# SwiGLU gate and up projections with seven block products for eight, and the down projection as its own stage

## The chip, the cores and the metric

The kernel runs on one core of one Trainium2 chip. The metric is device time in microseconds. The kernel before took 2962.8 us (median of three runs, 2962.63 to 2965.72). Engines: TensorE (PE) multiplies, VectorE (DVE) and ScalarE (ACT) do elementwise work, GpSimd (POOL) does a little of it, SyncE (SP) issues the transfers. PSUM is where TensorE accumulates.

## The reference

One decoder layer in fp32 with 2048 tokens, D = 1024 and D_FF = 2816, in three residual sub-layers. The change is in the third; the others are a hybrid token mixer and a cross-attention into 256 memory tokens.

```
hf = rmsnorm(x, g_ffn_pre)
ff = (jax.nn.silu(hf @ w_gate) * (hf @ w_up)) @ w_down
x = x + rmsnorm(ff, g_ffn_post)
```

## The kernel before

Every fp32 operand of a large product is split into two parts, hi and lo, in the format fp32r: `split` casts on ACT (L142) and subtracts on DVE or, where told, on POOL (L143). A product is then three passes, hi by hi, hi by lo and lo by hi (`PASS`), all into the same PSUM accumulation. A matmul has a 128x128 weight and 512 columns.

The stages follow one another: input projection, differential attention, output projection (`pmix`, L870), cross-attention over 16 token tiles (`psc` L1056, `pxo` L1095), and last SwiGLU, called the last stage here. The order on TensorE is written out by hand; that of ACT, DVE, POOL and SP is a scheduler's, which follows data and buffers.

The last stage works on two halves of 1024 tokens, and on 22 blocks f of 128 of D_FF. The tokens of a half are normalised (`d_load`, L126), turned by eight transposes (`d_turn`, L132) and split into `hfT` (L134, L135). For each f, `gate_up` loads a 512 KB block of w_gate and of w_up, splits each, and runs for each two groups (512 tokens) of 24 matmuls, 8 contraction blocks by 3 passes (`gu_mm`, L1173): 96 matmuls per f and half, 4224 in all. `gu_post` takes Silu on ACT (L1178), multiplies on DVE (L1179) and splits g, with POOL. After every two f's `down` multiplies g by two blocks of w_down (L1203, 96 matmuls: eight token tiles by two groups of six), and adds the result to y in SBUF (L1215). At the end of each half `down_end` does the last four f's, normalises y, adds the residual (POOL, L1263) and stores it, and in the first half turns the tokens of the second between its matmuls.

The first blocks are woven into the end of cross-attention: four token tiles are turned within its last two tokens, the four others between the first gate and up matmuls. Loads go through four buffers (`raw`, name `wr`), split weights through ten (`w4`), PSUM is four buffers of 1024 columns (`ps`). Pools are on the left side of SBUF, save those made with `right`: among them `vwp` (VW of cross-attention) and `yp` (y and g).

## Time and profile before

| what | us |
|---|---|
| median of three runs | 2962.8 |
| lowest and highest | 2962.63, 2965.72 |
| span of the profiled execution | 2962.6 |
| TensorE busy in it | 2879.2 (97%) |
| DVE busy | 1312.5 (44%) |
| ACT busy | 966.4 (33%) |
| POOL busy | 278.9 (9%) |
| last stage, first gate matmul to the end | 1481.6 to 2962.6 |

The profile is one execution; its span is the time from the first to the last instruction, and the median of the runs agrees with it. A matmul's own duration in it (390 ns for the gate and up matmuls) overlaps with its neighbours'; what a matmul costs is the pitch, the time of a run in the chain of waits divided by its count. The chain is followed back from the last instruction: each piece says who held the end at that time. Times below count from the start of the span.

### The profile page before, as it was taken

How to read it: one execution, taken by the hardware profiler on the slowest of the kernel's cores; microseconds unless marked ns; L12 is line 12 of the kernel's file. 1: busy time of each engine (PE TensorE's matmuls, PEld its weight loads, DVE VectorE, ACT ScalarE, POOL GpSimd, SP SyncE). 2: the span in 40 equal slices, each digit the busy share in tenths (PEclk: the TensorE clock that was granted, in tenths of full speed). 3: DMA queues.
4: the chain of work that ended last, by engine and by line, in shares of the span. 5: the costliest groups of instructions: out<-in, count | busy, mean ns of one | idle time of the engine just before them, and what ended most of it. 6: DMA issues, size and time to landing. Idle time of an engine off the chain costs nothing.

```text
span 2962.6 us, 34656 instructions
## 1 busy us (share of the span) xinstructions
PE 2879.2 (97%) x13948; PEld 2384.2 (80%) x13948; DVE 1312.5 (44%) x2069; ACT 966.4 (33%) x1986; POOL 278.9 (9%) x183
## 2 busy tenths in 40 slices
PE   9989999999889999999999999999999999999998
PEld 7778778888777888888878888888877888888887
DVE  4362378787885554333531332222263133222224
ACT  4232247677774443222322111111132211111112
POOL 0000012221221000000000000000021000000002
PEclk9999999999999999999999999999999999999999
DMA  5443473543433541111221111111143111111112
GB/s 181 137 162 107 158 222 108 150 141 106 134 100 119 192 172 44 44 50 47 92 96 50 43 44 57 50 50 49 44 143 113 50 43 45 56 50 50 50 43 100
DMA packets 217752, 273.48 MB, mean 92 GB/s; under 512 B 12280, under 2 KB 167032, under 8 KB 217592
## 3 DMA queue, kind: packets, MB, share of 16 engines
q1 hardware_dynamic: 217272, 270.22, 28.7%
q8 instruction: 110, 1.80, 0.3%
q0 software_dynamic: 320, 1.05, 0.1%
q14 instruction: 50, 0.41, 0.0%
HBM read 206.09 MB, written 65.14 MB: 92 GB/s over the span
## 4 chain that ended last, share of the span: by engine, by line
PE 81%; DVE 7%; DMA 2%; ACT 2%; issue 2%; POOL 1%; SPq 0%; DVEq 0%; ACTq 0%; POOLq 0%
PE pgu L1173 32%; PE pdn L1203 15%; PE pxo L1095 6%; PE psc L1056 6%; PE pmix L870 5%; PE S L731 3%; PE o L792 3%; PE pu L287 2%; DVE p L773 2%; PE pqk L287 2%; DVE nmx L738 2%; PE pv L303 1%; PE T L783 1%; PE S L870 1%; PE o L537 1%
## 5 line engine op out<-in xcount | busy, mean ns | idle before, releaser
L1173 PE MATMUL pgu<-hfT,w 128*128 128x512 f32 x4224 | 964.6, 390 | 3.3 <-DVE ms_y L106 2.0
L1173 PEld LDWEIGHTS pgu<-hfT,w 128*128 128x128 f32 x4224 | 793.4, 188 | 170.0 <-DVE ms_y L106 2.4
L1203 PE MATMUL pdn<-wd,g 128*128 128x512 f32 x2112 | 497.5, 396 | 2.2 <-ACT pdn L1260 2.2
L1203 PEld LDWEIGHTS pdn<-wd,g 128*128 128x128 f32 x2112 | 398.5, 189 | 95.5 <-ACT pdn L1260 2.6
L142 ACT CAST w<-wr 128x1024 fp32r<-128x1024 f32 (+2 forms) x208 | 134.4, 686 | 760.8 <-PE pgu L1173 414.0
L143 DVE TENSOR_TENSOR w<-wr,w 128x1024 fp32r<-128x1024 f32 (+2 forms) x206 | 156.8, 794 | 258.8 <-ACT w L142 245.1
L143 POOL TENSOR_TENSOR g<-sg,g 128x1024 fp32r<-128x1024 f32 x42 | 101.0, 2404 | 1745.5 <-ACT g L142 1745.5
L1179 DVE TENSOR_TENSOR sg<-pgu,sg 128x1024 f32<-128x1024 f32 x44 | 53.9, 1225 | 416.5 <-PE pgu L1173 416.5
L1215 DVE TENSOR_TENSOR y<-pdn,y 128x1024 f32<-128x1024 f32 x128 | 156.8, 1225 | 180.7 <-PE pdn L1203 180.7
L731 PE MATMUL S<-kt,q 128*128 128x512 f32 (+2 forms) x640 | 180.7, 397 | 34.3 <-ACT p L747 32.5
L747 ACT ACTIVATE p<-S,nmx 128x1024 f32<-128x1024 f32 (+3 forms) x192 | 167.7, 874 | 93.4 <-DVE nmx L740 39.1
L738 DVE TENSOR_REDUCE nmx<-S 128x1 f32<-128x1024 f32 (+3 forms) x192 | 173.4, 908 | 45.3 <-PE S L734 34.9
L1095 PE MATMUL pxo<-VW,pT 128*128 128x512 f32 x768 | 183.3, 397 | 0.4 <-ACT pT L142 0.4
L287 PE MATMUL pqk<-hT,w 128*128 128x512 f32 x768 | 179.3, 395 | 3.8 <-ACT w L142 3.8
L1056 PE MATMUL psc<-Mq,h 128*128 128x512 f32 x768 | 178.9, 392 | 0.0
L287 PEld LDWEIGHTS pqk<-hT,w 128*128 128x128 f32 x768 | 144.5, 188 | 38.3 <-ACT w L142 4.6
L1095 PEld LDWEIGHTS pxo<-VW,pT 128*128 128x128 f32 x768 | 143.1, 188 | 33.4 <-ACT pT L142 0.6
L1056 PEld LDWEIGHTS psc<-Mq,h 128*128 128x128 f32 x768 | 143.0, 188 | 29.3
L731 PEld LDWEIGHTS S<-kt,q 128*128 128x128 f32 x640 | 110.9, 195 | 58.8 <-ACT p L747 43.2
L870 PE MATMUL pmix<-wo,in 128*128 128x512 f32 x624 | 145.2, 394 | 0.0
L870 PEld LDWEIGHTS pmix<-wo,in 128*128 128x128 f32 x624 | 117.0, 188 | 27.6
L792 PE MATMUL o<-vt,aT 128*128 128x128 f32 x1088 | 136.5, 280 | 0.0
(257 smaller groups left out, 2883.8 us busy)
## 6 DMA issues: line engine op xcount, KB each, us to landing
wr<-in_w_gate SPq DMA_DIRECT2D x44, 512.0 KB
wr<-in_w_up SPq DMA_DIRECT2D x44, 512.0 KB
wr<-in_w_down SPq DMA_DIRECT2D x44, 512.0 KB
wr<-in_w_in SPq DMA_DIRECT2D x32, 512.0 KB
q<-qk_q SPq DMA_DIRECT2D x128, 128.0 KB
xt<-in_x SPq DMA_DIRECT2D x16, 512.0 KB
wr<-in_w_xkv SPq DMA_DIRECT2D x16, 512.0 KB
kt<-qk_k SPq DMA_DIRECT2D x16, 512.0 KB
```

Source lines behind the costliest of these rows:

```text
L143: (eng or v).tensor_tensor(dst_lo, src, dst_hi, ALU.subtract)
L287: pe.matmul(pt[:, ch * 512:(ch + 1) * 512], w[ws][:, k, :], hT[ch][hs][:, k, :], start=(n == 0), stop=(n == 23))
L731: pe.matmul(st[:, c0:c0 + cwm], x["qs"][s][:, m, q0:q0 + P], x["kst"][m][pc][:, c0:c0 + cwm], start=(s == 0), stop=(s == 1 and not last))
L738: v.tensor_reduce(nmx[:, pc:pc + 1], st[:, :w_], AX.X, ALU.max, negate=True)
L747: sc.activation(pt[:, :w_], st[:, :w_], AF.Exp, bias=nmx[:, pc:pc + 1], accum_out=x["l2"][:, m, pc:pc + 1])
L792: pe.matmul(ot[:, :P], aT[b // 4][:, (b % 4) * P:(b % 4 + 1) * P], vt[b // 8][:, b % 8, :], start=(b == 0), stop=(b == i))
L870: pe.matmul(pt[:, ch * 512:(ch + 1) * 512], iT[is_][:, k * P:(k + 1) * P], w[ws][:, ch * 512:(ch + 1) * 512], start=(n == 0), stop=(n == 23))
L1056: pe.matmul(pt[:, ch * 512:(ch + 1) * 512], h2[hs][:, k, :], Mq[k][ms_][:, ch * 512:(ch + 1) * 512], start=(n == 0), stop=(n == 23))
L1095: pe.matmul(pt[:, ch * 512:(ch + 1) * 512], pT[ps_][:, k, :], VW[k][vs][:, ch * 512:(ch + 1) * 512], start=(n == 0), stop=(n == 23))
L1173: pe.matmul(pt[:, ch * 512:(ch + 1) * 512], w[ws][:, k, :], hT[ch][hs][:, k, :], start=(n == 0), stop=(n == 23))
L1203: pe.matmul(pt[:, ch * 512:(ch + 1) * 512], gs[f][gi][:, t * P:(t + 1) * P], ws[f][wi][:, ch * 512:(ch + 1) * 512], start=(f == 0 and n == ...
L1215: v.tensor_tensor(y[t], pt, y[t], ALU.add)
```

## The change

The gate and up projections of one half are computed by one level of Strassen's scheme (in Winograd's form). Tokens are dealt into even and odd tiles, the contraction into its lower and upper 512, and two blocks of D_FF form a pair: a product of 2x2 blocks in seven block products, each of 4 contraction blocks by 3 passes, 12 matmuls of 512 columns for gate and 12 for up. The seven token operands, B11, T2, B21, T3, T1, T4 and B22 (`hc`), are built once for a half (`d_even`, `d_odd`). The seven weight operands are built for each pair (`weights`): four POOL additions per matrix and seven splits. Five DVE additions of 1024 columns combine the products; four times Silu and a product make g, which is stored unsplit in DRAM (`swiglu`, `g_d`).

The second half's operands are built during pairs 1 to 8 of the first (`d_even_kept`, `d_odd_kept`), kept unsplit in DRAM (`hc_d`), and loaded and split again at the change of halves, two loads (`hst`) for each operand through a buffer `st4`. The down projection runs after all tokens, in three parts of 8, 8 and 6 f's; in each part every token tile's g is loaded and split (`g_in`), and the products are added in 16 tiles y. Its number of matmuls is that of before. What lay in `dynamic_dma_scratch_size` is cut to 2048.

```diff
...
+    def d_even(hc, t):
+
+        pt = d_transposed(t)
+        for i, n in enumerate(("B11", "B21")):
+            put(hc, n, t % 8 // 2, pt[:, i * 512:(i + 1) * 512])
+        hf = ev.tile([P, T], F32, name="hf", tag="ev")
+        sc.copy(hf, pt)
+        return hf
+
+    def d_odd(hc, t, hf):
+
+        j = t % 8 // 2
+        pt = d_transposed(t)
+        h12 = w4t("h12", F32)
+        sc.copy(h12[:, 0:512], pt[:, 0:512])
+        t12 = w4t("t12", F32)
+        t1, t2 = t12[:, 0:512], t12[:, 512:]
+        v.tensor_tensor(t1, pt[:, 0:512], hf[:, 0:512], ALU.subtract)
+        v.tensor_tensor(t2, pt[:, 512:], t1, ALU.subtract)
+        put(hc, "T2", j, t2)
+        t3 = h12[:, 0:512]
+        v.tensor_tensor(t3, pt[:, 512:], t3, ALU.subtract)
+        put(hc, "T3", j, t3)
+        put(hc, "T1", j, t1)
+        t4 = h12[:, 512:]
+        gp.tensor_tensor(t4, t2, hf[:, 512:], ALU.subtract)
+        put(hc, "T4", j, t4)
+        put(hc, "B22", j, pt[:, 512:])
...
+    def d_odd_kept(t, hf):
+        j = t % 8 // 2
+        pt = d_transposed(t)
+        ho = w4t("ho", F32)
+        sc.copy(ho, pt)
+        keep("B22", j, ho[:, 512:])
+        t12 = w4t("t12", F32)
+        t1, t2 = t12[:, 0:512], t12[:, 512:]
+        gp.tensor_tensor(t1, ho[:, 0:512], hf[:, 0:512], ALU.subtract)
+        gp.tensor_tensor(t2, ho[:, 512:], t1, ALU.subtract)
+        gp.tensor_tensor(hf[:, 512:], t2, hf[:, 512:], ALU.subtract)
+        gp.tensor_tensor(hf[:, 0:512], ho[:, 512:], ho[:, 0:512], ALU.subtract)
+        keep("T1", j, t1)
+        keep("T2", j, t2)
+        keep("T4", j, hf[:, 512:])
+        keep("T3", j, hf[:, 0:512])
...
+    hpb = pool(esD, "hpb")
+    st4 = pool(esD, "st4", 1)
+    fh = pool(esD, "fh", 1)
+    half = pool(esD, "half", 3)
+    for n in HC:
+        if n not in hc:
+            hc[n] = hpb.tile([P, 2, 4, 512], F32R, name="h" + n)
+
+    def weights(wsrc, n):
+
+        ra, rb = [load_raw(wsrc[:, 4 * i:4 * i + 4, n * 256:n * 256 + 256], (P, 4, 256)) for i in range(2)]
+        a11, a21, a12, a22 = ra[:, :, 0:P], ra[:, :, P:], rb[:, :, 0:P], rb[:, :, P:]
+
+        def out(src):
+            w = w4t("w", F32R, (P, 2, 4, P))
+            split(w[:, 0], w[:, 1], src)
+            return w
+
+        s3 = half.tile([P, 4, P], F32, name="s3", tag="half")
+        gp.tensor_tensor(s3, a11, a21, ALU.subtract)
+        gp.tensor_tensor(a21, a21, a22, ALU.add)
+        yield out(a11)
+        gp.tensor_tensor(a11, a21, a11, ALU.subtract)
+        yield out(a11)
+        yield out(a12)
+        gp.tensor_tensor(a12, a12, a11, ALU.subtract)
+        yield out(s3)
+        yield out(a21)
+        yield out(a22)
+        yield out(a12)
+
+    def product(pt, i, w, h, start, stop):
+        n = 0
+        for (ws, hs) in PASS:
+            for k in range(4):
+                pe.matmul(pt[:, i * 512:(i + 1) * 512], w[:, ws, k, :], h[:, hs, k, :],
+                          start=(start and n == 0), stop=(n == 11),
+                          skip_group_check=not start)
+                n += 1
+
...
+    def pair(hv, n, hc, mids=()):
+        mids = dict(mids)
+        gens = [weights(w_, n) for w_ in (wg, wu)]
+        pts, s = {}, {}
+
+        def both(h, name, start, stop):
+            if start:
+                pts[name] = ps.tile([P, T], F32, name="pgu", tag="mm")
+            for i in range(2):
+                w = next(gens[i])
+                product(pts[name], i, w, hc[h], start, stop)
+                if (h, i) in mids:
+                    mids[h, i]()
+
...
+        f = 2 * n
+        both("B11", "X", True, False)
+        s["1"] = ev.tile([P, T], F32, name="s1", tag="ev")
+        sc.copy(s["1"], pts["X"])
+        both("T2", "Y", True, False)
+        s["16"] = ev.tile([P, T], F32, name="s16", tag="ev")
+        v.tensor_tensor(s["16"], pts["Y"], s["1"], ALU.add)
+        both("B21", "X", False, True)
+        sg = half.tile([P, 512], F32, name="sg", tag="half")
+        swiglu(*lo_hi(pts["X"]), hv, 0, f, sg)
+        both("T3", "Y", False, True)
+        v.tensor_tensor(s["1"], pts["Y"], s["1"], ALU.add)
+        both("T1", "Z", True, False)
+        c22 = ev.tile([P, T], F32, name="c22", tag="ev")
+        v.tensor_tensor(c22, pts["Z"], s["1"], ALU.add)
+        swiglu(*lo_hi(c22), hv, 1, f + 1, c22[:, 0:512])
+        both("T4", "W", True, True)
+        c21 = s["1"]
+        v.tensor_tensor(c21, c21, pts["W"], ALU.subtract)
+        swiglu(*lo_hi(c21), hv, 0, f + 1, c21[:, 0:512])
+        both("B22", "Z", False, True)
+        c12 = s["16"]
+        v.tensor_tensor(c12, pts["Z"], c12, ALU.add)
+        swiglu(*lo_hi(c12), hv, 1, f, c12[:, 0:512])
+
+    d_load(1)
+    d_load(3)
+
+    def odd_pair(x, y):
+        def go():
+            d_odd(hc, x, hfs.pop(x - 1))
+            if y is not None:
+                d_load(y)
+        return go
+
+    for n in range(NPAIR):
+        if n == 0:
+            pair(0, 0, hc, [(("B11", 0), odd_pair(1, 5)), (("B11", 1), lambda: (odd_pair(3, 7)(), odd_pair(5, None)(), odd_pair(7, 8)()))])
+            continue
+        if n <= 8:
+            t = 7 + n
+            if t % 2 == 0:
+                hfk = d_even_kept(t)
+            else:
+                d_odd_kept(t, hfk)
+            if t < NT - 1:
+                d_load(t + 1)
+        pair(0, n, hc)
+    hc = {}
+    for n in HC:
+        hc[n] = (hpa if n in ("B11", "B21") else hpb).tile([P, 2, 4, 512], F32R, name="h" + n)
+        for i in range(2):
+            st = st4.tile([P, 2, 512], F32, name="hst", tag="st4")
+            sp.dma_start(st, hc_d[n][:, 2 * i:2 * i + 2, :])
+            split(hc[n][:, 0, 2 * i:2 * i + 2, :], hc[n][:, 1, 2 * i:2 * i + 2, :], st)
+    for n in range(NPAIR):
+        pair(1, n, hc)
+    esD.close()
+
+
+    pin(sc.preload_act_table_set(LNEXP))
+    yp = pool(ctx, "ypD", 1)
+    wdp = pool(ctx, "wdp", 9)
     gfp = gain("g_ffn_post")
...
     def wdown(f):
         r_ = load_raw(a["w_down"][f * P:(f + 1) * P, :])
-        w = [w4t("wd") for _ in range(2)]
-        split(w[0], w[1], r_)
+        w = wdp.tile([P, 2, D], F32R, name="wd", tag="wd")
+        split(w[:, 0], w[:, 1], r_)
         return w
 
+    def g_in(p_, t):
+        nf = len(FPARTS[p_])
+        gr = tk.tile([P, nf, P], F32, name="gr", tag="tk")
+        sp.dma_start(gr, g_d[t // 8, t % 2, p_][t % 8 // 2])
+        gs = [w4t(f"g{s}", F32R, (P, nf, P)) for s in range(2)]
+        split(gs[0], gs[1], gr)
+        return gs
+
+    def down_mm(pt, gs, ws, f, ch):
+        for n, (gi, wi) in enumerate(PASS):
+            pe.matmul(pt[:, ch * 512:(ch + 1) * 512], gs[gi][:, f, :], ws[f][:, wi, ch * 512:(ch + 1) * 512],
+                      start=(f == 0 and n == 0), stop=(f == len(ws) - 1 and n == 2))
+
+    for p_, fs in enumerate(FPARTS):
         ws = [wdown(f) for f in fs]
-        for t in range(8):
+        L = len(ws)
+        for t in range(NT):
+            gs = g_in(p_, t)
             pt = ps.tile([P, T], F32, name="pdn", tag="mm")
-            down_mm(pt, t, gs, ws, range(len(fs)), True)
-            if first:
+            last = p_ == 2 and t == NT - 1
+            if last:
+                pt1 = ps.tile([P, T], F32, name="pdn", tag="mm")
+                for ch in range(2):
+                    for f in range(L):
+                        down_mm((pt, pt1)[ch], gs, ws, f, ch)
+            elif t in (0, NT - 1):
+                for f in range(L):
+                    for ch in range(2):
+                        down_mm(pt, gs, ws, f, ch)
+            else:
+                for ch in range(2):
+                    for f in range(L):
+                        down_mm(pt, gs, ws, f, ch)
+            if p_ == 0:
                 sc.copy(y[t], pt)
-            else:
+                continue
...
```

(The lines shown follow the diff; the functions that are taken out stand in the code above.)

The first place is the start of the last stage, on DVE. Before, behind the last cross-attention token (L1102, L1103):

```order
L1103 TENSOR_TENSOR xtC<-pxo,xtC 128x1024
L135 TENSOR_TENSOR hfT_13300<-pt,hfT_13299 128x8x128
L106 TENSOR_SCALAR ms_q<-ssq 128x1
L112 SCALAR_TENSOR_TENSOR e_q<-r_q,ms_q 128x1
L113 TENSOR_SCALAR e_q<-e_q 128x1
L115 TENSOR_TENSOR rx_142<-r_q,e_q 128x1
L126 SCALAR_TENSOR_TENSOR xtD<-xtD,rx_142,gain_g_ffn_pre 128x1024
L135 TENSOR_TENSOR hfT_13300<-pt,hfT_13299 128x8x128
L126 SCALAR_TENSOR_TENSOR xtD<-xtD,rx_142,gain_g_ffn_pre 128x1024
L135 TENSOR_TENSOR hfT_13300<-pt,hfT_13299 128x8x128 x2
L143 TENSOR_TENSOR w<-wr,w 128x1024
L1179 TENSOR_TENSOR sg<-pgu,sg 128x1024
```

Now, of four odd token tiles (`d_odd`: three additions and five splits each), the last and a part of the third, and what follows (`hT`, `hB` are operands of tokens, `w<-wr` the low parts of weights, among them the first for T2):

```order
L143 TENSOR_TENSOR hT_13574<-h_13696,hT_13574 128x4x128
L143 TENSOR_TENSOR hT_13576<-h_13696,hT_13576 128x4x128
L143 TENSOR_TENSOR hB_13577<-pt,hB_13577 128x4x128
L1162 TENSOR_TENSOR t_13724<-pt,t_13724 128x512
L1165 TENSOR_TENSOR h_13722<-pt,h_13722 128x512
L143 TENSOR_TENSOR hT_13575<-t_13724,hT_13575 128x4x128
L143 TENSOR_TENSOR hT_13573<-t_13724,hT_13573 128x4x128
L143 TENSOR_TENSOR hT_13574<-h_13722,hT_13574 128x4x128
L143 TENSOR_TENSOR hT_13576<-h_13722,hT_13576 128x4x128
L143 TENSOR_TENSOR hB_13577<-pt,hB_13577 128x4x128
L126 SCALAR_TENSOR_TENSOR xtD<-xtD,rx_142,gain_g_ffn_pre 128x1024
L143 TENSOR_TENSOR w<-wr,w 128x512 x4
```

Token work that came one subtraction at a time between the gate matmuls stands now as a block ahead of the weights' low parts.

The second place is the boundary between the pairs 1 and 2 on ACT. Before, between two blocks f (`sg` is the Silu, `w<-wr` the casts of the next weights):

```order
L1178 ACTIVATE sg<-pgu 128x1024
L142 CAST w<-wr 128x1024
L142 CAST g_13821<-sg 128x1024
L142 CAST w<-wr 128x1024
L1178 ACTIVATE sg<-pgu 128x1024
L142 CAST w<-wr 128x1024
L142 CAST g_13938<-sg 128x1024
```

Now (the four `L1280` rows are the Silus of the four g of pair 1; `ho` is the copy of an odd tile of the second half; the casts behind are those of pair 2):

```order
L142 CAST w<-wr 128x512 x3
L1280 ACTIVATE sg<-pgu 128x512
L1280 ACTIVATE c_14147<-c_14147 128x512
L1280 ACTIVATE s_14012<-s_14012 128x512
L1188 COPY ho<-pt 128x1024
L1280 ACTIVATE s_14047<-s_14047 128x512
L142 CAST w<-wr 128x512 x6
L142 CAST w<-s_14250 128x512
L142 CAST w<-s_14272 128x512
```

The first cast of the next weights was ahead of the Silu, and it stands now behind the last Silu of the pair here.

The third place is SP's queue at the change of halves. Before (`xtD` are the token tiles of the second half, `wr` weights, and residuals x):

```order
L1117 DMA xtD<-x_8_133 128x1024
L1117 DMA xtD<-x_9_134 128x1024
L508 DMA wr<-x_3_128 128x1024
L1117 DMA xtD<-x_10_135 128x1024
L1117 DMA xtD<-x_11_136 128x1024
L1117 DMA xtD<-x_12_137 128x1024
L1117 DMA xtD<-x_13_138 128x1024
L1264 DMA out<-y_13536 128x1024
L508 DMA wr<-x_4_129 128x1024
L1264 DMA out<-y_13537 128x1024
L508 DMA wr<-x_5_130 128x1024
L1117 DMA xtD<-x_14_139 128x1024
```

Now (`hst` are halves of the operands of the second half, `g` stores):

```order
L1356 DMA hst<-hc_T_10720 128x1024
L1283 DMA g_10709<-sg 128x4x128
L1356 DMA hst<-hc_T_10720 128x1024
L1356 DMA hst<-hc_B_10721 128x1024
L1283 DMA g_10712<-c_16574 128x4x128
L1356 DMA hst<-hc_B_10721 128x1024
L1283 DMA g_10709<-s_16439 128x4x128
L1356 DMA hst<-hc_T_10722 128x1024
L508 DMA wr<-in_w_gate 128x4x256 x2
L1283 DMA g_10712<-s_16474 128x4x128
L1356 DMA hst<-hc_T_10722 128x1024
L1356 DMA hst<-hc_T_10723 128x1024
```

Eight token loads became 14 loads of operands, all in one buffer, with weights and stores between them.

## Rows read from the trace of the kernel before

**Rows 1.** The page: its first line and its part 1 (busy time by engine).
```profile
span 2962.6 us, 34656 instructions
PE 2879.2 (97%) x13948; PEld 2384.2 (80%) x13948; DVE 1312.5 (44%) x2069; ACT 966.4 (33%) x1986; POOL 278.9 (9%) x183
```

**Rows 2.** The chain of waits, last stage: start us, us, what.
```profile
1553.65 22.32 PE pdn L1203 x96
1575.97 43.56 PE pgu L1173 x192
...
2908.64 41.84 PE pdn L1203 x180
```

**Rows 3.** Windows of both halves: us, busy us (instructions) by engine, clock, DMA share, GB/s.
```profile
1504.00:2168.00 664.00, 663.62 (x2904) 545.71 (x2905) 179.00 (x149) 117.64 (x114) 50.49 (x21) 1.00 0.17 50
...
2240.00:2908.00 668.00, 668.00 (x2925) 549.33 (x2924) 176.31 (x147) 115.65 (x112) 50.50 (x21) 1.00 0.17 52
```

**Rows 4.** The chain of waits: one token of cross-attention.
```profile
1431.40 11.19 PE pxo L1095 x48
```

**Rows 5.** Groups by line and shape: busy us, mean ns | idle before, releasers.
```profile
L143 POOL TENSOR_TENSOR g<-sg,g 128x1024 fp32r<-128x1024 f32 x42 | 101.0, 2404 | 1745.5 <-ACT g L142 1745.5
...
L1215 DVE TENSOR_TENSOR y<-pdn,y 128x1024 f32<-128x1024 f32 x128 | 156.8, 1225 | 180.7 <-PE pdn L1203 180.7
...
L142 ACT CAST wd<-wr 128x1024 fp32r<-128x1024 f32 x44 | 46.3, 1052 | 203.2 <-issue 127.2 <-PE pgu L1173 76.0
...
L126 DVE SCALAR_TENSOR_TENSOR xtD<-xtD,rx,gain_g_ffn_pre 128x1024 f32<-128x1024 f32 x16 | 20.4, 1280 | 14.4 <-DMA xtD<-x 14.4
...
L143 DVE TENSOR_TENSOR pw<-o,pw 128x512 fp32r<-128x512 f32 x16 | 11.0, 688 | 7.3 <-ACT pw L142 7.2
...
L142 ACT CAST pw<-o 128x512 fp32r<-128x512 f32 x16 | 9.5, 594 | 0.9 <-PE o L563 0.9
```

**Rows 6.** Timelines of PE and DVE, and the chain, where the last stage starts.
```profile
1481.57 5.62 PE L1173 MATMUL pgu<-hfT,w 128*128 128x512 f32 x24
...
1504.38 10.96 PE L1173 MATMUL pgu<-hfT,w 128*128 128x512 f32 x47 [1.10 <-ACT hfT L134]
...
1487.03 1.23 DVE L1103 TENSOR_TENSOR xtC<-pxo,xtC 128x1024 f32<-128x1024 f32 x1
...
1488.66 7.40 DMA xtD<-x
```

**Rows 7.** Timeline of PE behind two idle stretches, and the window behind the first.
```profile
178.37 1.94 PE L132 MATMUL pt<-cst,xn 128*128 128x128 f32 x8 [8.52 <-DVE xn L126]
179.96 12.77 PE L287 MATMUL pu<-hT,w 128*128 128x512 f32 x48
...
193.36 11.39 PE L287 MATMUL pu<-hT,w 128*128 128x512 f32 x48
...
2216.01 7.39 PE L1203 MATMUL pdn<-wd,g 128*128 128x512 f32 x24 [2.24 <-ACT pdn L1260]
...
178.00:182.00 4.00, 3.63 (x13) 3.28 (x14) 3.96 (x7) 1.40 (x2) 0.50 (x1) 0.50 0.68 231
```

**Rows 8.** The change of halves: windows, and two loads in the chain.
```profile
2168.27:2234.10 65.83, 61.40 (x289) 49.61 (x288) 52.58 (x63) 24.90 (x43) 18.81 (x7) 0.97 0.53 169
2212.00:2216.00 4.00, 1.77 (x12) 1.31 (x11) 3.56 (x4) 1.15 (x2) 0.10 (x1) 1.00 0.83 256
...
2181.20 4.33 DMA xtD<-x
...
2221.45 4.75 DMA wr<-in_w_up
```

**Rows 9.** Timeline of POOL and DVE at the end of the run.
```profile
2951.24 0.69 DVE L1250 TENSOR_TENSOR yg<-y,gain_g_ffn_post 128x512 f32<-128x512 f32 x1
...
2953.59 2.34 POOL L1263 TENSOR_TENSOR y<-y,wr 128x1024 f32<-128x1024 f32 x1 [3.28 <-DVE y L1262]
...
2954.14 2.33 DVE L1250 TENSOR_TENSOR yg<-y,gain_g_ffn_post 128x512 f32<-128x512 f32 x1
```

More of the change, by code (lines that the diff above doesn't have):

```diff
@@ L1110, in layer @@
     NF = FF // P
+    NPAIR = NF // 2
     wg = a["w_gate"].rearrange("(k p) c -> p k c", p=P)
     wu = a["w_up"].rearrange("(k p) c -> p k c", p=P)
+    FPARTS = (range(0, 8), range(8, 16), range(16, NF))
+    HC = ("B11", "T2", "B21", "T3", "T1", "T4", "B22")
+    g_d = {(hv, odd, p_): dram.tile([4, P, len(fs), P], F32, name=f"g_{hv}{odd}{p_}")
+           for hv in range(2) for odd in range(2) for p_, fs in enumerate(FPARTS)}
+    hc_d = {c_: dram.tile([P, 4, 512], F32, name=f"hc_{c_}") for c_ in HC}
     dn = {}
@@ L1145, in layer @@
             esM.close()
-            hp = pool(ctx, "hpD", 1)
+            esD = ExitStack()
+            hpa = pool(esD, "hpa")
+            ev = pool(esD, "ev", 4)
             gf = gain("g_ffn_pre")
-            hT = [[hp.tile([P, KD, 512], F32R, name=f"hfT{c}{s}") for s in range(2)] for c in range(2)]
+            hc = {n: hpa.tile([P, 2, 4, 512], F32R, name="h" + n) for n in ("B11", "B21")}
             d_load(0)
-            d_load(1)
-        d0 = 2 * (t - NT + 2)
-        d_turn(hT, d0)
@@ new lines, in product, with swiglu @@
+    def product(pt, i, w, h, start, stop):
[6 more added lines that the diff above has]
+                n += 1
+    def swiglu(gate, up, hv, odd, f, dst):
+        sc.activation(dst, gate, AF.Silu)
+        v.tensor_tensor(dst, up, dst, ALU.mult)
+        p_ = f // 8
+        sp.dma_start(g_d[hv, odd, p_][:, :, f - FPARTS[p_][0], :].rearrange("t p c -> p t c"),
+                     dst.rearrange("p (t c) -> p t c", t=4))
@@ L1192, in wdown @@
+    wdp = pool(ctx, "wdp", 9)
+    gfp = gain("g_ffn_post")
+    y = [yp.tile([P, D], F32, name=f"y{t}") for t in range(NT)]
     def wdown(f):
         r_ = load_raw(a["w_down"][f * P:(f + 1) * P, :])
-        w = [w4t("wd") for _ in range(2)]
-        split(w[0], w[1], r_)
-        return w
-    def down_mm(pt, t, gs, ws, fs, last, chs=(0, 1)):
-        for ch in chs:
-            n = 0
-            for f in fs:
-                for (gi, wi) in PASS:
-                    pe.matmul(pt[:, ch * 512:(ch + 1) * 512], gs[f][gi][:, t * P:(t + 1) * P], ws[f][wi][:, ch * 512:(ch + 1) * 512],
-                              start=(f == 0 and n == 0), stop=(last and f == fs[-1] and n == 2))
-                    n = (n + 1) % 3
@@ L1241, in down_end @@
+            xr = load_raw(x2_d[t])
+            o_ = out[0, t * P:(t + 1) * P, :]
+            if last:
                 ss = small.tile([P, 2], F32, name="ss2")
```

141 lines of the change are left out of this document (36 added, 105 removed).

## The prediction

> **What bounds the kernel now.** I read the page's busy line first: TensorE is busy for 2879.2 of 2962.6 us [rows 1], so only fewer matmuls, shorter matmuls or shorter holes in TensorE's work can move the end. The chain of waits is read next. In the last stage it alternates between 192 gate and up matmuls in 43.56 us and 96 down matmuls in 22.32 us [rows 2], with nothing between: a pitch of 226.9 ns and of 232.5 ns. The windows over the middle of each half show the same, 663.62 busy of 664 and 668.00 of 668, with VectorE (DVE) at 179 and 176, ScalarE (ACT) at 118 and 116, GpSimd (POOL) at 50, and the DMA engines at a share of 0.17 [rows 3]. There are 4224 gate and up matmuls, which is 4224 x 226.9 ns = 958 us of pure TensorE time, in a stage where the other engines are three quarters idle. The sum below is made against the profiled span of 2962.6 us; the median of the three runs, 2962.8, is the same for this purpose.
>
> **Matmuls removed.** A pair of blocks in one half took 2 blocks x 2 matrices x 48 = 192 matmuls. It now takes 7 products x 2 x 12 = 168. Over 11 pairs and 2 halves that is 528 fewer, of unchanged shape: 528 x 226.9 ns = **-119.8 us** (a). The 2112 down matmuls and the 128 transposes of tokens stay.
>
> **Their pitch.** The trace has two pitches for one shape. Where both operands lie in pools on the left side the pitch is 226.9. Where one lies in a pool on the right (g in the down projection, VW in cross-attention) it is 232.5 and 233.1 (11.19 / 48) [rows 2, 4]. The after program puts the tiles of T1, T4 and B22 at the addresses that VW held. I take the higher pitch for 3 of 7 products: 1584 x 5.6 ns = **+8.9 us** (b), bounds 0 and +10. For the down stage g moves left and most of wd right, so I leave 232.5: 0 (c). All at 226.9 would give -11.8, all at 233.1 +1.3.
>
> **Work that is added beside the matmuls.** A pair now costs 14 casts on ACT and 14 subtractions on DVE of 512 columns, five DVE additions of 1024 columns from PSUM, four products of 512 columns, and eight POOL operations. With 0.69 us for a 512-column DVE operation and 1.22 for one of 1024 [rows 5], DVE needs 14 x 0.69 + 5 x 1.22 + 4 x 0.69 = 18.5 us. ACT needs 14 x 0.59 + 1.05 + 4 x 0.59 = 11.7. POOL, at half of 2404 ns, needs 9.6. TensorE needs 168 x 0.23 = 38.6 us for the same pair. So in the middle of a half all of this hides, as does the traffic of g through DRAM (22 blocks x 1 MB out and back over some 1400 us, beside a share of 0.17). I cost it at nothing there. Without that cover it would be DVE and POOL one after the other, 28 us, still under 38.6. What does not hide lies at four seams.
>
> **Start of the last stage.** TensorE ends cross-attention at 1481.57, and DVE ends the last cross-attention token at 1487.03 + 1.23 = 1488.26 [rows 6]. In the order of the changed program DVE then has, ahead of the low part of the first T2 weight, all four odd tiles: 4 x 8 operations of 512 columns (22.1 us), three token normalisations (1.28 each, 3.8), two weight parts (1.4) and small ones (0.8), at the durations of [rows 5]: 28.1, so T2 can start at 1516.4. TensorE has only the B11 product (24 x 0.227 = 5.4) and four tiles of transposes (eight took 179.96 - 178.37 = 1.59 at half the clock [rows 7], so 0.8 a tile: 3.2) and is done at 1490.2. It waits 26.2 us. The loads of tokens 5 and 7 stand behind the last store as before (7.40 us from 1488.66) and arrive within this time. After an idle TensorE comes a slow stretch: after 8.52 us of idling the granted clock was 0.50 of 2.4 GHz, eight transposes took 1.94 us and 48 matmuls 12.77 instead of 11.39, about 2.3 us lost; after 2.24 us, 24 matmuls took 7.39, about 1.6 lost [rows 7]. I add 2.3. Before, this place lost 22.81 - (72 x 0.227 + 3.2) = 3.3 us between 1481.57 and 1504.38 [rows 6]. Net **+25.2 us** (d), bounds +16 (ACT and DVE overlap better, loads early) and +33.
>
> **Boundaries between pairs.** While the second half's tokens are prepared (pairs 1 to 8), ACT's order at four boundaries is: the copy of an odd tile (ho), the Silu of the last block product, and only then the cast of the next pair's first weight. That Silu needs the DVE addition on the last matmul. So TensorE waits for 1.22 (addition) + 0.59 (Silu, priced as the 512-column cast) + 0.59 (cast) = 2.4 us, some 0.3 of hand-overs, and 1.6 of slow clock [rows 5, 7]: 4.3 x 4 = **+17.2 us** (e), bounds +10 and +22. At the other boundaries the cast stands some ten half-products ahead of its use, and costs nothing.
>
> **Half switch.** The seven token tiles of the second half come back as 14 loads of 512 KB through one buffer, each with a cast (1.05) and a subtraction (1.22) [rows 5] before the next load may start. The nearest rows have 4.33 and 4.75 us for such a load at the end of a chain [rows 8], so a step takes 6.6 to 7.0 us. The first load is early and the first tile comes free 5.5 us into the last pair of the first half, so the last is ready near 94 to 99 us, where TensorE would want it at 38.6 + 33 = 71.7. That is 22 to 27 us. At the 256 GB/s that a window of this place moved [rows 8], a load would take 2.0 us, a step 4.3, and there would be no wait. I take 20, near the rows, plus 3 for the clock. What goes is the old switch: 65.83 us [rows 8] for 192 x 0.2325 + 6.4 (eight tiles of transposes) + 32 x 0.227 = 58.3, thus 7.5. Net **+15.5 us** (f), bounds -6 and +23.
>
> **Start of the down stage.** Its first weights are split behind the last addition, Silu and product of the last pair, 1.22 us of DVE for each of eight blocks, against 48 matmuls of the first tile. About **+4.5 us** with the clock (g), bounds 0 and +9. Later parts have nine buffers and splits well ahead; the last tile and its tail are the same code.
>
> **A rule against it.** At the end of the run a DVE operation of 512 columns with two SBUF inputs took 2.33 us while a POOL addition of 2.34 ran, against 0.69 for its twin just before [rows 9]. The Trainium skill, page "SBUF — State Buffer", section "SBUF: two separate sides", says that such a DVE operation and a GpSimd operation that reads SBUF lock a shared port for the whole instruction, so one blocks the other; the trace agrees, 2.33 against 0.69. The change puts POOL operations into (d) and (f). If each of some four of them in the start held DVE up by its 1.2 us, and some seven at the switch, the sum would be 5 + 8 us longer, 2927; that is a rival below.
>
> **The sum.** -119.8 + 8.9 + 0 + 25.2 + 17.2 + 15.5 + 4.5 = -48.5; 2962.6 - 48.5 = **2914 us**.
>
> **Rivals.**
> 1. *Seams mostly hidden.* If reloads run at the rate of the window, (f) is -6 and (d) +16, and the pitch of the down stage falls to 226.9, the sum is -119.8 + 8.9 - 11.8 + 16 + 17 - 6 + 2 = -94: 2869; with one or two of these only, about 2885. For it: 4.33 is the end of a chain that includes the issue, not a transfer alone. Against: the order shows one buffer and DVE's 28 us. Chance 0.13 (2865 to 2895).
> 2. *Locked port and slow reloads*, each seam at its upper end or the lock above: 2927 to 2955. For it: [rows 9]. Against: many DVE operations there read PSUM. Its part over 2935: chance 0.15.
> 3. *Slower than before: weights late at every boundary.* Each pair needs 14 split weights in ten buffers and both load buffers of a matrix until its last product. If the next pair's first weight is then late everywhere by the 4.3 us of (e), the 17 other boundaries add 73 us: 2987. It decides from 48.5 / 17 = 2.9 us at each. For it: four raw buffers hold exactly one pair. Against: a weight's buffer returns after four of 14 half-products, which leaves some 25 us for a load of 4.75 and a split. Chance 0.09.
> 4. *The products don't go faster.* Groups of 12 matmuls, with two accumulations into a bank, could have a longer pitch. At 48.5 us / 3696, that is 13 ns more than here, all gain is gone. Against: down groups of six run at 232.5 [rows 2]. Chance 0.05, around 2962.
>
> **Numbers.** The forecast itself (2895 to 2935) has 0.58. I give the range 2872 to 2955, which leaves out the lowest of rival 1 and rivals 3 and 4. The measurement can tell about 0.2% (6 us) from no change. Faster: 0.58 + 0.13 + 0.15 = 0.86; same 0.05; slower 0.09.
>
> **What would show it.** In the changed profile: 3696 gate and up matmuls, and a pair's chain of 168 in about 38.6 us with two pitches by tile; TensorE idle some 26 us behind the B11 product with DVE as releaser (d); four holes of 2.4 to 3 us released by ACT's cast (e); at the switch waits that grow from T3 to B22, ended by DVE's subtraction behind a load (f); and no hole at the other boundaries. The forecast is wrong if the pitch of short groups rises, if boundaries stall everywhere, or if the reload is much quicker or slower than 6.8 us a step.

## The result, and the profile after

The changed kernel takes 2897.6 us (median of four runs, 2894.0 to 2900.8) against 2962.7: a ratio of 0.9778, 95% interval 0.9764 to 0.9792, so 65 us less. The forecast was 2914, range 2872 to 2955. The sum was 16 us too long, and most of its terms can be read one by one in the trace. The profiled execution is the slowest of the four: a span of 2899.0 us. The first lines of the page, and the chain of waits in the last stage (start us, us, what):

```profile
span 2899.0 us, 35143 instructions
PE 2767.6 (95%) x13420; PEld 2293.9 (79%) x13420; DVE 1510.5 (52%) x2393; ACT 1087.7 (38%) x2294; POOL 464.1 (16%) x337
```

```profile
1522.51 31.09 PE pgu L1273 x136
1554.48 38.13 PE pgu L1273 x168
...
1601.00 2.25 POOL wr L1260
1603.94 32.94 PE pgu L1273 x144
...
1958.88 3.62 DMA hst<-hc_B
1964.86 4.23 DMA hst<-hc_T
...
2011.74 3.63 DMA hst<-hc_B
2016.50 388.97 PE pgu L1273 x1702
2411.89 6.24 DMA wr<-in_w_down
2420.51 470.64 PE pdn L1385 x2075
```

Where [rows 2] alternated between gate and up and down, there are two long blocks now. 168 gate and up matmuls take 38.1 us, and 2075 down matmuls take 470.64 us, 226.8 ns each. Between the blocks the chain leaves TensorE in four kinds of place: at the start, at some boundaries of pairs, at the change of halves (the `hst` loads) and at the start of the down stage. The middle of a half and the down stage have no hole; the other engines are busier than in [rows 3], but far from full (windows as there: us, then busy us of PE, PEld, DVE, ACT and POOL, clock, DMA share, GB/s):

```profile
2024.00:2405.00 381.00, 381.00 (x1682) 315.48 (x1682) 190.01 (x225) 120.94 (x188) 105.08 (x72) 1.00 0.29 87
2425.00:2885.00 460.00, 460.00 (x2031) 380.91 (x2030) 126.45 (x157) 90.50 (x128) 33.58 (x14) 1.00 0.26 88
```

From the first gate matmul to the end, the last stage took 2962.6 - 1481.6 = 1481.0 us before, and takes 2899.0 - 1488.05 = 1410.9 now: 70.1 less. The stages ahead of it ended 6.5 us later in this execution. Their code is the same; the other profiles with the same early stages (the runs below without padding) reached the first gate matmul between 1483.5 and 1490.3, so part of this is scatter between executions. With the padding that is tried below, the kernel before gets there at 1474.2 and the changed kernels between 1470.1 and 1475.6, so no systematic difference is seen.

The losses of the last stage, each the time beyond 226.9 ns a matmul, from the start times of the matmuls:

| place | forecast | measured |
|---|---|---|
| start, pair 0 (without its transposes) | 28.5 | 24.1 |
| boundaries, pairs 1 to 8 (without transposes) | 17.2 | 21.4 |
| change of halves, pair 11 | 23 | 24.1 |
| the 12 other pairs | 0 | 0 |
| start of the down stage | 4.5 | 6.5 |

One more difference stands behind the last matmul: from there to the end it took 2962.6 - (2908.64 + 41.84) = 12.12 us before [rows 2], and takes 2899.0 - (2420.51 + 470.64) = 7.85 now. The DVE operation of 2.33 us in [rows 9] is not in the chain any more.

### The profile page after: what moved, and what is told of

Its sections match the earlier page's. It is cut to its first block, busy times and chain, and to the rows that moved or that the text cites. A ratio compares the mean times of both kernels' runs of the same rounds, so it can differ in the third digit from the quotient of the medians.

```text
span 2899.0 us, 35143 instructions
## 1 busy us (share of the span) xinstructions
PE 2767.6 (95%) x13420; PEld 2293.9 (79%) x13420; DVE 1510.5 (52%) x2393; ACT 1087.7 (38%) x2294; POOL 464.1 (16%) x337
## 3 DMA queue, kind: packets, MB, share of 16 engines
q8 instruction: 106, 1.74, 0.3%
## 4 chain that ended last, share of the span: by engine, by line
PE 78%; DVE 8%; DMA 4%; ACT 3%; issue 1%; POOL 1%; SPq 0%; DVEq 0%; ACTq 0%; POOLq 0%
PE pgu L1273 26%; PE pdn L1385 16%; PE pxo L1095 6%; PE psc L1056 6%; PE pmix L870 5%; PE S L731 3%; PE o L792 3%; PE pu L287 2%; DVE p L773 2%; DVE nmx L738 2%; PE pv L303 2%; PE T L783 1%; PE pqk L287 1%; PE o L537 1%; PE S L870 1%
## 5 line engine op out<-in xcount | busy, mean ns | idle before, releaser
L1273 PE MATMUL pgu<-hT,w 128*128 128x512 f32 x2112 | 495.3, 394 | 27.6 <-ACT hT L142 21.0
L1273 PEld LDWEIGHTS pgu<-hT,w 128*128 128x128 f32 x2112 | 400.9, 190 | 115.8 <-ACT hT L142 22.3
L1385 PE MATMUL pdn<-wd,g 128*128 128x512 f32 x2112 | 481.7, 390 | 4.2 <-DVE wd L143 3.5
L1273 PE MATMUL pgu<-hB,w 128*128 128x512 f32 x1584 | 375.0, 394 | 16.5 <-ACT w L142 10.0
L143 DVE TENSOR_TENSOR w<-wr,w 128x512 fp32r<-128x512 f32 (+3 forms) x382 | 260.3, 707 | 214.7 <-ACT w L142 213.8
L1273 PEld LDWEIGHTS pgu<-hB,w 128*128 128x128 f32 x1584 | 299.5, 190 | 82.2 <-ACT w L142 11.2
L142 ACT CAST w<-wr 128x512 fp32r<-128x512 f32 (+3 forms) x384 | 202.0, 557 | 343.7 <-PE pgu L1273 206.4
L1257 POOL TENSOR_TENSOR s<-wr 128x512 f32<-128x512 f32 x44 | 62.3, 1416 | 878.1 <-PE pxo L1095 524.9
L142 ACT CAST g<-gr 128x1024 fp32r<-128x1024 f32 (+1 forms) x48 | 47.1, 982 | 338.5 <-PE pdn L1385 301.4
```

The source lines that it names most:

```text
L142: sc.copy(dst_hi, src)
L143: (eng or v).tensor_tensor(dst_lo, src, dst_hi, ALU.subtract)
L1273: pe.matmul(pt[:, i * 512:(i + 1) * 512], w[:, ws, k, :], h[:, hs, k, :], start=(start and n == 0), stop=(n == 11), skip_group_check=not s ...
L1385: pe.matmul(pt[:, ch * 512:(ch + 1) * 512], gs[gi][:, f, :], ws[f][:, wi, ch * 512:(ch + 1) * 512], start=(f == 0 and n == 0), stop=(f == ...
```

## The experiments

All but the first edit the changed kernel. Each time stands beside runs of the kernel before on the same chip (medians of 2964 to 2967 us), so the ratios carry the comparisons; by its ratio the changed kernel would take 2900 there. Labels in brackets, as (e1), name the runs.

**The pitch.** The forecast gave 3 of 7 products the slow pitch, since T1, T4 and B22 lie where VW had been, and left the down stage at 232.5. Both are wrong: every product runs at 226.7, and down too. The addresses of the tiles in the two programs, which no view of a trace shows, follow another pattern: all pools on the left side stand at 352 bytes modulo 512 in a partition, all on the right at 480. The slow matmuls of before are those with one operand on each side. Two edits tell this apart from the side itself. The first pads the left side, for the kernel before (and for the changed one):

```diff
+    const.tile([P, 32], F32, name="pad")
     cst = const.tile([P, 2 * P + 65], F32, name="cst")
```

> The kernel before with an unused tile of 128 bytes a partition ahead of all pools on the left side; nothing else. It moves every left pool from 352 to 480 bytes modulo 512, where the pools on the right side stand. Theory A (a matmul is slower where the offsets of its two operands modulo 512 differ, 352 and 480): the down matmuls go from 232.5 to 226.7 ns (2112 x 5.8 = 12.2 us), cross-attention's second product from 233.1 to 226.7 (768 x 6.4 = 4.9), the output projection from 231.9 to 226.7 (624 x 5.2 = 3.2): about 20 us less, 2942. Theory B (an operand at 480 is slow by itself): gate and up (4224) and all others go to 232.5, at least 24 us more, above 2985. Theory C (the step of my prediction: the right side, or high addresses, make a matmul slow): no change, 2963.

Measured (e1): 2942.1 us, ratio 0.9916 (0.9901 to 0.9931). The kernel before becomes 24 us faster by 128 unused bytes. The chain of waits has for the output projection before:

```profile
951.07 133.60 PE pmix L870 x576
```

and with the padding, beside [rows 2, 4]:

```profile
951.54 130.56 PE pmix L871 x576
...
1118.34 10.92 PE pxo L1096 x48
...
2822.95 65.28 PE pgu L1174 x288
2888.23 10.89 PE pdn L1204 x48
```

The output projection goes from 133.60 us (the same 576 matmuls, 231.9 ns each) to 130.56, 226.7 each; 48 matmuls of cross-attention from 11.19 to 10.92; 48 of the down projection take 10.89, 226.9 each. Gate and up stay at 65.28 / 288 = 226.7, though both their operands now stand at 480. That is theory A: not the side, not the height, not an offset by itself, but a difference between the offsets. The two profiles show the 20 us expected: 7.9 between the first matmul of the output projection and the first gate matmul (530.7 before, 522.8 now), and 12.0 in the down projection. The input projection, which I had left out, has a lower pitch too (a median of 227 instead of 232 ns), but between its first and last matmul the profiles don't show the gain, 245 us before and 248 here; where the other 4 us come from is open.

> The changed kernel with the same unused tile of 128 bytes. Theory A: gate, up and down stay at 226.7 ns, since both operands move; cross-attention's second product and the output projection become 226.7: 8 us less than the changed kernel, about 2889. Theory B: gate, up and down go to 232.5, 5808 x 5.8 = 34 us more, 2931. Theory C: no change, 2898.

Measured (e2): 2883.3, ratio 0.9722 (0.9705 to 0.9738), against 0.9778 for the changed kernel: some 16 us less. Gate, up and down stayed at 226.7 to 226.9; cross-attention's second product and the output projection joined them (523.4 us from the first output-projection matmul to the first gate matmul, 530.5 in the changed kernel). That is 7 of the 8 us expected; the rest lies further ahead, where the pitch of the input projection fell too, and where profiles of the same code differ by several us.

The second edit moves one operand alone:

```diff
+    yp.tile([P, 32], F32, name="pad")
     wdp = pool(ctx, "wdp", 9)
```

> The changed kernel with 128 unused bytes ahead of the pool of w_down's tiles alone, so that wd stands at 480 modulo 512 and g at 352; no other operand of a matmul moves. Theory A: the down matmuls go from 226.7 to 232.4, 2112 x 5.7 = 12 us more, 2910. Theory C, or no effect of offsets: 2898.

Measured (e3): 2908.7, ratio 0.9802 (0.9786 to 0.9819): 11 us over the changed kernel's median, 7 by the ratios, whose intervals overlap a little (0.9764 to 0.9792 for the changed kernel). The chain's last line decides:

```profile
2418.11 482.47 PE pdn L1386 x2075
```

The same 2075 matmuls take 482.47 us instead of 470.64: 232.5 ns each, 11.8 us more. The slow pitch is back with 128 bytes between the operands. Only the residues 352 and 480 were tried, so what other differences cost is open, and so is whether 512 is the right modulus.

**The boundaries of pairs.** In the changed kernel, at the boundary of pairs 1 and 2 (PE, then ACT, then POOL; in brackets the idle time before and what ended it):

```profile
1592.45 1.03 PE L1133 MATMUL pt<-cst,xtD 128*128 128x128 f32 x8
1595.68 7.37 PE L1273 MATMUL pgu<-hB,w 128*128 128x512 f32 x24 [2.19 <-ACT w L142]
1603.94 5.74 PE L1273 MATMUL pgu<-hT,w 128*128 128x512 f32 x24 [0.89 <-ACT w L142]
```

```profile
1593.58 1.01 ACT L1188 COPY ho<-pt 128x1024 f32<-128x1024 f32 x1 [4.49 <-PE pt L1133]
1594.48 0.63 ACT L1280 ACTIVATE s<-s 128x512 f32<-128x512 f32 x1
1595.02 1.13 ACT L142 CAST w<-wr 128x512 fp32r<-128x512 f32 x2
1603.27 0.62 ACT L142 CAST w<-wr 128x512 fp32r<-128x512 f32 x1 [7.12 <-POOL wr L1260]
```

```profile
1594.66 1.27 POOL L1192 TENSOR_TENSOR t<-ho,hf 128x512 f32<-128x512 f32 x1 [22.32 <-ACT ho L1188]
...
1600.96 3.50 POOL L1260 TENSOR_TENSOR wr<-wr 128x512 f32<-128x512 f32 x2
```

ACT was idle for 4.49 us, then copied ho, did the Silu, and only then the cast that TensorE waited for, with 2.19 us of idling. The copy came last because it waits for the tile's transposes on TensorE; DVE's addition for that Silu was over at 1593.87. The 24 matmuls behind the hole took 7.37 us instead of 5.60. The granted clock was 0.54 there, but it was 1.00 behind the same hole at the next boundary (windows as above):

```profile
1595.70:1599.40 3.70, 3.70 (x9) 2.94 (x10) 3.70 (x3) 0.44 (x1) 3.62 (x4) 0.54 0.72 233
1678.95:1682.60 3.65, 3.20 (x13) 2.33 (x14) 3.65 (x3) 0.45 (x1) 3.57 (x4) 1.00 0.95 297
```

Then comes a second hole: POOL does four differences of the odd tile ahead of the weight for T2. At the four boundaries the T2 holes are 0.89, 1.77, 0.82 and 0.83 us of idling. The first edit takes ho and t12 out of the ring of the split weights:

```diff
-        ho = w4t("ho", F32)
+        ho = st4.tile([P, T], F32, name="ho", tag="st4")
...
-        t12 = w4t("t12", F32)
+        t12 = ev.tile([P, T], F32, name="t12", tag="ev")
```

> The changed kernel; the copy of an odd kept tile (ho) and its differences (t12) are taken from the pools st4 and ev instead of w4, the ring of the split weights. Theory ring: the casts of the next pair's weights stand behind the copy of ho because they come after it in w4's ring, so with another pool all holes at the boundaries of pairs 1 to 8 close (21.4 us in the changed kernel without the transposes): 2876. Rival POOL: the holes come from the four POOL operations on the kept tiles ahead of the weights' additions; those stay, so only the cast's part goes (four holes of 2.2 us and their slow clock, some 15 us), and a T2 hole of 0.9 to 1.7 us remains at each: about 2883.

Measured (e5): 2875.3, ratio 0.9691 (0.9677 to 0.9705). The losses of pairs 1 to 8 fall from 21.4 us to 0.6 without the transposes; the same boundary on PE:

```profile
1589.20 1.04 PE L1133 MATMUL pt<-cst,xtD 128*128 128x128 f32 x8
1589.99 5.71 PE L1273 MATMUL pgu<-hB,w 128*128 128x512 f32 x24
1595.55 5.60 PE L1273 MATMUL pgu<-hT,w 128*128 128x512 f32 x24
```

POOL still does the same four differences, but in the program's order its additions for these weights now come ahead of them. So the cause of both holes is the ring: weights that come after ho in it were split after ho. That ho and t12 leave two buffers fewer for weights is not the reason by itself: in the changed kernel ACT casts no weight between 1566.1 and 1595.0, while TensorE is done with another one every 2.7 us (12 matmuls). Here the casts follow at that step, and the last two stand ahead of ho:

```profile
1586.73 0.62 ACT L142 CAST w<-wr 128x512 fp32r<-128x512 f32 x1 [0.89 <-PE pgu L1273]
1589.45 0.62 ACT L142 CAST w<-wr 128x512 fp32r<-128x512 f32 x1 [2.10 <-PE pgu L1273]
1590.27 1.02 ACT L1188 COPY ho<-pt 128x1024 f32<-128x1024 f32 x1 [0.20 <-PE pt L1133]
```

The other edit keeps the ring and moves the four differences to DVE (`gp` to `v` in `d_odd_kept`):

> The changed kernel; the four additions on a kept odd tile run on DVE instead of POOL, their buffers and places stay. Theory: the T2 holes (0.9 to 1.7 us and the slow clock behind them) come from POOL, where the next pair's weight additions stand behind these four, and go; the B11 holes of 2.2 us come from ACT's order and stay. Some 4 to 8 us less than the changed kernel: 2892. If the whole boundary is POOL's, 20 us less: 2877. If POOL has no part in it: 2898 or somewhat more.

Measured (e5b): 2892.5, ratio 0.9752 (0.9735 to 0.9768). The T2 hole is gone, the B11 hole is there, as expected:

```profile
1594.67 7.36 PE L1273 MATMUL pgu<-hB,w 128*128 128x512 f32 x24 [2.19 <-ACT w L142]
1601.87 5.60 PE L1273 MATMUL pgu<-hT,w 128*128 128x512 f32 x24
```

The losses of pairs 1 to 8 are 16.8 us here, 4.6 less than the 21.4; the idling of the four T2 holes alone was 4.3. POOL's part is only roughly that, for the clock differs: here it was slow behind all four B11 holes (0.54 to 0.56), and in six other profiles that leave this place alone the boundaries lose between 19.8 and 23.1 us.

**The change of halves.** PE in pair 11 of the changed kernel, and the queue of SP:

```profile
1990.91 7.81 PE L1273 MATMUL pgu<-hT,w 128*128 128x512 f32 x24 [5.17 <-ACT hT L142]
2004.16 7.57 PE L1273 MATMUL pgu<-hT,w 128*128 128x512 f32 x22 [5.43 <-ACT hT L142]
...
2016.50 9.75 PE L1273 MATMUL pgu<-hB,w 128*128 128x512 f32 x29 [4.31 <-ACT hB L142]
```

Three operands in a row, T1, T4 and B22, are late by about 5 us, each with a slow stretch behind it: 7.5, 8.0 and 7.5 us lost. Of the 24.1 us, 15.7 are idling and the rest is slow clock. A load takes 3.6 to 4.2 us in the chain, not the 4.33 to 4.75 of [rows 8], and a step from load to load 5.9 to 6.9 (1958.88 to 1964.86 is one). Two steps take 8.2 and 7.3, since the cast of a loaded half stands on ACT behind the cast of a weight. The edit lets the second half of each operand go through another buffer:

```diff
-            st = st4.tile([P, 2, 512], F32, name="hst", tag="st4")
+            st = (st4, fh)[i].tile([P, 2, 512], F32, name="hst", tag=("st4", "hf")[i])
```

> The changed kernel; the second of the two loads of each operand at the change of halves goes to the buffer fh, which is free by then, instead of st4: two loads may run at once. Theory one buffer: a step of load, cast and subtraction of 6.0 to 6.4 us, 14 of them in a row, makes the 24 us lost in pair 11; with two buffers the seven operands take about 45 us, under the 66 that TensorE gives them, and 20 to 24 us go: 2875. Rival queue: weights and stores of g wait behind these loads on SP, and the splits behind each other on ACT and DVE; then half of the loss stays, 2886.

Measured (e4): 2876.5, ratio 0.9697 (0.9683 to 0.9712). The loss of pair 11 falls from 24.1 to 2.7 us; what is left stands at the front of the pair:

```profile
1969.24 5.73 PE L1273 MATMUL pgu<-hB,w 128*128 128x512 f32 x24 [1.51 <-ACT s L1306]
1975.62 16.61 PE L1273 MATMUL pgu<-hT,w 128*128 128x512 f32 x72 [0.65 <-DVE s L1309]
```

The single buffer was the cause; the queue of SP and the casts of weights, which were left as they were, cost no more than these 2.7 us without it.

**The start.** PE of the changed kernel, and a window over the wait:

```profile
1488.05 2.90 PE L1273 MATMUL pgu<-hB,w 128*128 128x512 f32 x12
...
1502.97 3.73 PE L1133 MATMUL pt<-cst,xtD 128*128 128x128 f32 x16 [4.87 <-DVE xtD L126]
1517.11 3.88 PE L1273 MATMUL pgu<-hT,w 128*128 128x512 f32 x8 [10.40 <-ACT hT L142]
1522.51 3.90 PE L1273 MATMUL pgu<-hT,w 128*128 128x512 f32 x16 [1.52 <-DVE w L143]
```

```profile
1494.70:1517.10 22.40, 6.25 (x30) 4.75 (x29) 22.35 (x36) 16.52 (x32) 6.18 (x6) 0.70 0.49 163
```

DVE is busy for 22.35 of 22.40 us. From the end of the last cross-attention token on DVE to the low part of the T2 weight, behind which the 16 matmuls at 1522.51 start, it has no gap either:

```profile
1494.77:1522.47 27.70, 10.06 (x38) 7.07 (x36) 27.65 (x43) 20.20 (x38) 6.77 (x5) 0.69 0.40 131
```

Three edits tried to shorten the wait. In seven profiles that leave the start as it is, pair 0 loses 28.1 to 30.3 us, transposes included; that is the scatter to compare with. The first lets pair 0 do B21 ahead of T2, in `pair` and in the order of `weights`:

```diff
+        if first:
+            both("B21", "X", False, True)
         both("T2", "Y", True, False)
```

> The changed kernel; in the first pair of the first half alone the product B21 runs ahead of T2 (its operands need no odd tile). Theory: the start waits for DVE, which has all four odd tiles ahead of the first T2 product, so 24 matmuls (5.4 us) of the wait of 24 us are filled: 2892. Rival: the wait moves to B21, whose weight stands behind the same work on ACT and DVE, and nothing is gained: 2898.

Measured (e6): 2902.6, ratio 0.9787 (0.9773 to 0.9802), no gain; the loss of pair 0 is 35.0 us instead of 28.1 (transposes included). The rival holds:

```profile
1511.69 2.80 PE L1277 MATMUL pgu<-hB,w 128*128 128x512 f32 x8 [2.58 <-ACT w L142]
1524.93 6.28 PE L1277 MATMUL pgu<-hB,w 128*128 128x512 f32 x16 [10.44 <-DVE w L143]
```

B21 gets its hi part, and stops at the low part, which DVE does behind all odd tiles. The second edit writes the odd tiles' work in two parts (`d_odd_a` up to T2, the other operands from a function called behind B21):

```diff
+        put(hc, "T2", j, t2)
+
+        def b():
+            gp.tensor_tensor(hf[:, 512:], t2, hf[:, 512:], ALU.subtract)
...
+            (("B21", 1), lambda: [b() for b in late])
```

> The changed kernel; the work on the four first odd tiles is written in two parts: the copy, two differences and the split of T2 for all four tiles ahead of the T2 product, the operands T3, T1, T4 and B22 behind the B21 product (the first tile's ho and t12 come from st4 and fh). No operation is left out, one copy per tile is twice as wide. Theory order: TensorE's wait at the start is the number of DVE operations that stand ahead of the last T2 operand and weight; in the new order they are 21 of 512 columns and three of 1024, 19 us instead of 28, so the loss in pair 0 falls by about 8 us: 2890. Rival: the operands left for later are then late for B21, T3 or T1, and the wait comes back there: 2895 to 2900.

Measured (e7): 2898.4, ratio 0.9778 (0.9761 to 0.9794), no gain. T2 starts 26.3 us after the first gate matmul instead of 29.1, and T4 and B22 lose 3.5 and 1.5 us that they had not lost; pair 0 loses 30.0 in all. Again the rival, though the wait came back at T4 and B22 and not at B21, T3 or T1. The third takes work from DVE:

```diff
-        put(hc, "T1", j, t1)
+        put_act(hc, "T1", j, t1)
```

(and so for T4 and B22. `put_act` leaves out the low part: it casts the whole value on ACT a second time, in its place. So it is a probe of time, and no kernel to keep.)

> The changed kernel; for the first half's odd tiles the low parts of T1, T4 and B22 are written by a cast on ACT instead of the subtraction on DVE (this leaves out these low parts, so that 12 DVE operations of 0.69 us become 12 of ACT of 0.6). Theory DVE: the wait at the start is DVE's work on the odd tiles, not the late loads of tokens 5 and 7; 12 x 0.69 = 8.3 us of it go, so the loss of 28 us in pair 0 falls to 20 to 22: 2891. Rival loads: the loads and the chain behind them set the wait, and it stays at 26 to 28: 2897. Rival ACT: ACT, with 7 us more, becomes the bound, and it stays or grows.

Measured (e8): 2892.6, ratio 0.9756 (0.9739 to 0.9772); pair 0 loses 26.3 us, 1.8 less than in the changed kernel, where DVE's theory wanted 6 to 8; the first T2 matmul comes 28.9 us after the first gate matmul, as against 29.1. The median is near the 2891 of DVE's theory by luck: in the profiles 4.3 of the difference stand ahead of the last stage, whose first gate matmul comes at 1483.8 instead of 1488.05.

```profile
1490.50:1513.00 22.50, 6.64 (x31) 5.08 (x30) 21.09 (x31) 19.34 (x37) 6.06 (x6) 0.63 0.47 161
```

In the corresponding window DVE is still busy for 21.09 of 22.50 us, since normalisations of later tokens moved up into the room (five L126 operations instead of two), and ACT went from 16.52 to 19.34. So taking work from DVE did not shorten its queue by as much, and two engines are nearly full. That the wait comes back elsewhere when order alone changes is shown twice; what a shorter queue on DVE would give by itself is left open.

**Together.** Three combinations, each with the padding, two buffers and the free ring:

> The changed kernel with the 128 bytes of padding, two buffers at the change of halves, ho and t12 out of the weights' ring, and B21 ahead of T2 in the first pair. If the four theories hold and add up: 2897.6 - 8 - 21 - 22 - 5 = about 2841. If two of the seams share a cause, or the holes move elsewhere, 2850 to 2865.

Measured (best1): 2850.0, ratio 0.9610 (0.9595 to 0.9624); the sum of the four theories is missed by 9 us, and with e6's order its pair 0 loses 36.1.

> The changed kernel with the 128 bytes of padding, two buffers at the change of halves, ho and t12 of the kept tiles out of the weights' ring, and the two-part work on the first odd tiles; B21 is in its old place. By the runs so far, best1 (2850) had a loss of 36 us in pair 0 where the changed kernel has 28, so going back gives 8, and the two-part order another 8 if its theory holds: about 2834. If the wait at the start only moves: 2842.

Measured (best2): 2848.2, ratio 0.9606 (0.9592 to 0.9620), over both values expected; pair 0 loses 30.2.

> The changed kernel with the 128 bytes of padding, two buffers at the change of halves, and ho and t12 of the kept tiles out of the weights' ring; the start as in the changed kernel. Its loss in pair 0 should be 28 us, against 36 in best1 and 30 in best2: 2846, 2 us under best2, which is at the edge of what the runs can tell; if the start's loss is the same sum of DVE's work in whatever order, 2848.

Measured (best3): 2847.3, ratio 0.9602 (0.9587 to 0.9617); pair 0 loses 29.5, the boundaries 0.6, pair 11 2.6. The three can't be told apart. They are about 50 us under the changed kernel and 118 under the kernel before, and the simplest, best3, is the one to keep: by the losses in its trace the ring is worth 20.8 us and the buffers 21.4, and with the padding the first gate matmul comes at 1475.1, some 11 us earlier than in the middle of the unpadded profiles; that is the 52 us of the ratios. The two orders at the start add nothing.

## Why the prediction was right, and where its steps failed

**Matmuls removed (a).** Right to a fraction: an undisturbed pair takes 38.08 us, 168 x 226.7 ns, where 192 took 43.56; 22 x 5.48 = 120.6 us against 119.8.

**Pitch (b, c).** This is the step that failed. The rows were read correctly, two pitches for one shape, but the reason given, the place (left or right side, high addresses), was one of several that fitted. Forecast +8.9 and 0; measured 0 and 2112 x 5.7 = -12. Together 21 us, more than the whole error. The -11.8 was in the text as a bound. The trace of before could not tell them apart, but the changed program could have warned: the tiles of T1, T4 and B22 stand high, where VW stood, yet at 352 like the weights and not at 480. In place of the step: the slow pitch of 232.5 ns goes with a difference of 128 bytes between the offsets of the operands, and the pitch is 226.7 without it, on whichever side they lie (e1, e3).

**Start (d).** The arithmetic of DVE's queue gave 28.1 us, thus 26.2 of waiting, and 2.3 for the clock; measured 24.1 in all. DVE's queue holds just the operations that were listed, and took 27.7 us without a gap. In that sum two errors cancel, which is luck: DVE starts an operation of 512 columns every 0.60 us where the sum had 0.69, and some operations take longer beside POOL (below). Most of the other 4 us are missing because eight T2 matmuls, which don't need the low part of the weight, ran within the wait, and the clock was up again behind it (16 matmuls in 3.73 us). That less work for DVE shortens the wait by as much is not shown: e8 took 8.3 us away, and other work moved in.

**Boundaries (e).** Four holes at the places and with the releaser that were named, ACT's cast. The path to it was another: the Silu waited for the copy of ho behind the tile's transposes, and not for DVE's addition, so the idling was 2.19 us at each and not 2.7. The slow clock, put at 1.6 behind each, was there behind one of these four holes, and behind the T2 hole of 1.77. And the sum had no term for POOL, whose order makes the T2 holes, 4.3 us of idling (e5b). So 5.3 us each instead of 4.3 is near by errors of both signs. The cause, which the prediction only described as ACT's order, is the ring (e5).

**Half switch (f).** Forecast 23, measured 24.1, for the reason given (e4). The parts were off and made up for each other: 20 of waiting and 3 of clock became 15.7 and 8.4, as there are three slow stretches. The step of 6.6 to 7.0 us was mostly 5.9 to 6.9. The waits were said to grow from T3 to B22 and to end with DVE's subtraction; they begin at T1, are about equal, and end with ACT's cast.

**Down stage (g).** 6.5 instead of 4.5: the loads of w_down came late (6.24 us in the chain), not only the splits.

**The tail.** The prediction put it at nothing, as the same code. It is 4.3 us shorter, 7.85 instead of 12.12, and that too made the sum too long.

**The rivals.** The first needed a reload of 2.0 us; it took 3.6 to 4.2. The second, a locked port, is there, but it adds less than the rival wanted at the start. In the groups by form (mean ns after the comma), the same subtraction of 512 columns has two prices:

```profile
L143 DVE TENSOR_TENSOR hT<-t,hT 128x512 fp32r<-128x512 f32 x8 | 7.4, 956 | 0.0
...
L143 DVE TENSOR_TENSOR hT<-h,hT 128x512 fp32r<-128x512 f32 x8 | 5.2, 680 | 0.1
```

The eight splits from t are those of T2 and T1. The mean hides two kinds: three of the four T2 splits take 1.38 us, beside the POOL operation of 1.27 that forms T4 (the one at 1505.74 starts while POOL works from 1505.30), one takes 0.81, and T1's take 0.68. That is 2.2 us in all, where the rival had 5. The Trainium skill, page "SBUF — State Buffer", section "SBUF: two separate sides", says that a DVE operation with two SBUF inputs and a GpSimd operation that reads SBUF exclude each other for a whole instruction; the trace agrees, 1.38 against 0.68. At the boundary of pairs 1 and 2 it shows again: two splits of w take 3.44 us from 1596.40 on, beside POOL's differences of 1.60 to 1.74. What part of the T2 hole this makes, no run separates. The third rival, weights late at all boundaries, did not come: 12 pairs lose nothing. The fourth did not either: groups of 12 run at 226.7 ns.

The errors were of both signs: -21 for the pitch, -0.8 for the matmuls removed, -4.4, +4.2, +1.1 and +2.0 for the seams, -4.3 for the tail, and +6.5 ahead of the last stage. They add up to -16.7, against -15 for the profiled execution. The range held them; that the seams came within 5 us each is in part luck, as their parts show.

## What to carry to other kernels

A change that removes work from the bounding engine is worth what it removes less the seams, and seams can be priced beforehand: write down, for each place where the order is not steady, what the slowest queue has ahead of the first thing that engine needs. A buffer ring shared by two kinds of tiles also orders the work on them, so a tile that comes late should not stand in the ring of tiles that are needed early (21 us here). Where rows of one shape have two prices, ask what else differs between them than the one thing that comes to mind, and compare the addresses too.
